# Linear attention on one core: loads of K and V in pairs of groups, and stores that wait for a load directly

## The chip, the cores and the metric

The kernel runs on one core of a Trainium2 chip. The core has five engines with instruction streams of their own: PE (matrix multiply, with its weight loads shown as PEld), DVE (vector), ACT (scalar), POOL (GpSimd) and SP (sync, which only issues transfers here). Sixteen DMA engines move data between HBM and the on-chip memory SBUF. POOL, SP and ACT each issue transfers; POOL's go to the queue q0, SP's to q1 and ACT's to q10. The metric is the device time of one execution in microseconds (us); less is better. MB below are 1,048,576 bytes where a tile is meant.

## The reference

```python
Q_feat = np.maximum(0, Q)
K_feat = np.maximum(0, K)
KV = np.einsum('bhkd,bhkv->bhdv', K_feat, V)
K_sum = np.sum(K_feat, axis=2)
numerator = np.einsum('bhqd,bhdv->bhqv', Q_feat, KV)
denominator = np.einsum('bhqd,bhd->bhq', Q_feat, K_sum)
return (numerator / (denominator[:, :, :, None] + 1e-10)).astype(np.float32)
```

Q, K, V and the result are fp32 of shape 8 x 12 x 512 x 64: 96 heads, each 512 rows of 64 numbers, 12.58 million bytes per tensor.

## The kernel before

**Tiling.** The 96 heads are cut into 12 octets of 8 heads (`NO = 12`); each octet has two groups of 4 heads. For a group, K is a tile of 128 partitions with 16 rows of 64 numbers each, so 4 KB of fp32 in one piece per partition and 512 KB in all; V likewise. For an octet, Q is a tile with 8 KB per partition, 1 MB in all, and so is the output. An octet therefore reads 3 MB by five loads (K, V, K, V, Q) and writes 1 MB by one store.

**Loads.** All loads except those of the first octet's K and V are issued by POOL (lines 92 to 100, loop at 110) and change fp32 to bf16 on the way, so they write half the bytes they read. The order on POOL is Q of octet 0, then for each octet K and V of group one, K and V of group two, and Q. The four K and V tiles of the first octet are loaded as fp32 by SP (K) and ACT (V), lines 103 to 107; they lie in two buffers of the output pool. The pools `kin` and `vin` have 12 buffers each (one group per buffer, six octets), `qin` has 7 (one octet each), and `outp` has `DELAY + 2` = 7. In the compiled program a POOL load also waits for the landing of the load eight before it, so at most eight POOL loads are under way.

**Compute.** `prep` and `prep_v` (lines 133 to 146) make masked copies of K (with relu) and V of one group on DVE and ACT; `mm_kv` (148) multiplies them on PE; `evac_kv` (156) copies the products to SBUF on ACT. `qt` (181) transposes Q on PE and applies relu on ACT. `denom` (207) and `out_t` (193) form the denominators and the numerators, `backs` (272) transposes the numerators back on PE, divides them on DVE into an output tile `o_sb` (`norm`, line 234) and calls `store`. The work is issued in the order written (`manual_schedule`), in a loop over octets (lines 286 to 301) that prepares octet o+1 while it finishes octet o and, up to octet 8, octet o-1. From `o >= SAME = 8` the order differs: octet o is finished in the same round.

**Stores.** `store(o)` (line 240) is issued by SP. It first issues a copy of one row of 64 numbers from the K tile of octet o + `DELAY` into `scratch`. That copy can't leave until this K tile has landed, and as SP issues in order, the store behind it can't either. So stores of early octets are held back until the load stream is five octets further on. The last five octets' stores have no such copy. The last octet's store is cut into two halves (line 245).

Of the kernel before, what the change touches and what calls it, by code (L numbers as in the profile page):

```python
# [10 lines left out]
def kernel(  # L11
# [7 lines left out]
    nc = tc.nc  # L19
    B, H, S, D = Q.shape  # L20
    assert D == 64
    P = 128
# [4 lines left out]
    R = S * 4 // P  # L27
# [3 lines left out]
    NG = NH // NHG  # L31
    NO = NG // 2
    assert NO * 8 == NH and R == 16 and RQ == 32
    DELAY = 5
    F32 = 2

    fp32 = mybir.dt.float32
    bf16 = mybir.dt.bfloat16
# [3 lines left out]
    def pool(name, bufs, **kw):  # L42
        return ctx.enter_context(tc.tile_pool(name=name, bufs=bufs, **kw))

    consts = pool("consts", 1)
    qin = pool("qin", 7)
    kin = pool("kin", 12)
    vin = pool("vin", 12)
    kfp = pool("kfp", 4)
    rcp = pool("rcp", 2)  # L50
    outp = pool("outp", DELAY + 2)
    otp = pool("otp", 2)
# [5 lines left out]
    def view(X, f):  # L58
        return X.rearrange("b h s d -> (b h s d)").rearrange("(n p f) -> n p f", p=P, f=f)

    Qr, Kr, Vr, Or = view(Q, RQ * D), view(K, R * D), view(V, R * D), view(out, RQ * D)
# [14 lines left out]
    kvf = [consts.tile([P, 8 * 2 * D1], bf16, name=f"kvd{i}") for i in range(NK)]  # L76
    kvd = [x.rearrange("p (h d) -> p h d", h=8) for x in kvf]
    mask = consts.tile([P, 2, 2], fp32, name="mask")
    scratch = consts.tile([1, D], bf16, name="scratch")

    mask_h = consts.tile([P, 8, 2], fp32, name="mask_h")

# [5 lines left out]
    ctx.enter_context(tc.manual_schedule())  # L88

    q_sb, k_sb, v_sb = {}, {}, {}  # L90

    def load_kv(g):
        k_sb[g] = kin.tile([P, R, D], bf16, name="k_sb")
        nc.gpsimd.dma_start(out=k_sb[g].rearrange("p r d -> p (r d)"), in_=Kr[g])  # L94
        v_sb[g] = vin.tile([P, R, D], bf16, name="v_sb")
        nc.gpsimd.dma_start(out=v_sb[g].rearrange("p r d -> p (r d)"), in_=Vr[g])  # L96

    def load_q(o):
        q_sb[o] = qin.tile([P, U, 2 * D], bf16, name="q_sb")
        nc.gpsimd.dma_start(out=q_sb[o].rearrange("p u f -> p (u f)"), in_=Qr[o])  # L100


    for g in range(F32):
        kv = outp.tile([P, 2, R, D], fp32, name="kv_first", tag="o_sb")
        k_sb[g], v_sb[g] = kv[:, 0], kv[:, 1]
        nc.sync.dma_start(out=k_sb[g].rearrange("p r d -> p (r d)"), in_=Kr[g])
        nc.scalar.dma_start(out=v_sb[g].rearrange("p r d -> p (r d)"), in_=Vr[g])
    load_q(0)
    make_identity(nc, ident)
    for o in range(1, NO):  # L110
        load_kv(2 * o)
        load_kv(2 * o + 1)
        load_q(o)

    def zero(i):
# [122 lines left out]


    def store(o, o_sb):  # L240
        if o + DELAY < NO:
            nc.sync.dma_start(out=scratch, in_=k_sb[2 * (o + DELAY)][0:1, 0, :])
        Ov = Or[o].rearrange("p (r d) -> p r d", d=D)
        if o == NO - 1:
            for j in range(2):
                rs = slice(RQ // 2 * j, RQ // 2 * (j + 1))
                nc.sync.dma_start(out=Ov[:, rs], in_=o_sb[:, rs])
            return
        nc.sync.dma_start(out=Ov, in_=o_sb)

    def out_tile():
        return outp.tile([P, RQ, D], fp32, name="o_sb", tag="o_sb")
# [19 lines left out]
    def backs(o):  # L272
        o_sb = out_tile()
        for j in range(2):
            norm(o, j, back(o, j), o_sb)
        store(o, o_sb)
# [26 lines left out]
    o = NO - 2  # L303
    g = 2 * NO - 2
# [9 lines left out]
    o_sb = out_tile()  # L314
# [4 lines left out]
    for i in range(2):  # L319
        relu_q(o + 1, i, transp(o + 1, i), nc.vector if i == 1 else None)  # L320
    norm(o, 1, ps, o_sb)
    store(o, o_sb)
    idle(5, o + 1)
    out_t(o + 1, (0,))
# [32 lines left out]
```

## Time and profile before

Three runs took 126.52, 126.65 and 126.98 us; the median is 126.65. The profiled execution has a span of 124.8 us from its first to its last instruction; the runs' times include what lies around the span.

| what | value |
|---|---|
| median of three runs | 126.65 us |
| span of the profiled execution | 124.8 us |
| read from HBM, written to HBM | 37.75 MB, 12.58 MB |
| loads of Q, K, V by POOL (q0) | 12 + 22 + 22 |
| transfers on SP: first K, small copies, stores | 2 + 7 + 13 |
| transfers on ACT: first V | 2 |
| POOL busy | 31.2 us |
| issue to landing, median: K, V, Q loads | 14.1, 13.2, 14.8 us |
| issue to landing, median: whole stores | 9.0 us |

In the profile's slices each digit is a fortieth of the span; in the windows the last three columns are the clock granted to PE, the share of the 16 DMA engines' time that had packets in it (it can exceed 1, as packets overlap), and GB/s on the side written. In a timeline the first column is the start, the second the duration, and the bracket says how long the engine stood idle before and what ended that.

### The profile page before, as it was taken

To read this page: it belongs to the slowest core of one execution; us is meant where nothing else is said; L and a number is where in the kernel's file an instruction comes from. 1 tells how busy PE (TensorE), PEld (TensorE's weight loads), DVE (VectorE), ACT (ScalarE), POOL (GpSimd) and SP (SyncE) were. 2 spreads that over 40 slices of the span, in tenths; PEclk is the share of its full clock that TensorE was granted. 3 is DMA by queue.
4 is the path that set the end of the run, shared out by engine and by line. 5 is a ranking of instruction groups with operands and counts; after the bars stand their busy time and mean duration, and the time that the engine had idled before them with its cause. 6 is when DMAs were issued, how large, how long until landed. Compare 5 with 4: busy or idle time off the path is not lost.

```text
span 124.8 us, 2656 instructions
## 1 busy us (share of the span) xinstructions
PE 86.6 (69%) x1067; PEld 78.5 (63%) x1067; DVE 81.1 (65%) x176; ACT 79.4 (64%) x114; POOL 31.2 (25%) x62
## 2 busy tenths in 40 slices
PE   0032287998889899893598599399777577797600
PEld 0031285997878787792597499299576476695500
DVE  2257644759797997989147845934928918979430
ACT  0163369989898999988149558665939737737100
POOL 6902434314243331142133115034122000000000
PEclk9999999999999999999779859959999999999995
DMA  3999999999999999999999999999999999999993
GB/s 112 377 306 215 215 205 210 217 205 218 203 215 211 206 223 324 253 216 300 281 215 280 304 213 249 331 215 230 334 234 218 323 257 215 312 421 420 428 416 143
DMA packets 10748, 32.68 MB, mean 262 GB/s; under 512 B 1392, under 2 KB 1392, under 8 KB 9328
## 3 DMA queue, kind: packets, MB, share of 16 engines
q0 software_dynamic: 8064, 17.83, 74.7%
q1 hardware_dynamic: 2384, 13.63, 27.1%
q10 hardware_dynamic: 288, 1.05, 2.2%
q8 instruction: 8, 0.13, 0.4%
q14 instruction: 4, 0.03, 0.1%
HBM read 37.75 MB, written 12.58 MB: 403 GB/s over the span
## 4 chain that ended last, share of the span: by engine, by line
DMA 34%; DVE 30%; PE 23%; ACT 5%; issue 2%; DVEq 1%; SPq 0%; POOLq 0%; ACTq 0%
DMA v_sb<-in_V_dram 14%; DVE o_sb L234 13%; DMA q_sb<-in_Q_dram 13%; PE ps_kv L150 11%; DMA kv_first<-in_K_dram 7%; PE ps_bk L228 7%; DVE kf L136 5%; PE ps_qt L171 4%; DVE vo L138 3%; ACT kvd L160 2%; DVE vo L145 2%; PE ps_ot L201 2%; DVE den L218 2%; ACT qt L179 2%; DVE rec L222 1%
## 5 line engine op out<-in xcount | busy, mean ns | idle before, releaser
L150 PE MATMUL ps_kv<-vo,kf 128*128 128x132 bf16 x384 | 30.8, 244 | 17.7 <-ACT vo L143 8.2
L150 PEld LDWEIGHTS <-kf 128*128 128x128 bf16 x384 | 28.4, 110 | 19.0 <-DVE vo L138 10.9
L234 DVE TENSOR_TENSOR o_sb<-ps_bk,rec 128x1024 f32<-128x1024 f32 x24 | 28.3, 1219 | 17.1 <-PE ps_bk L228 17.1
L160 ACT CAST kvd<-ps_kv 64x260 bf16<-64x260 f32 (+1 forms) x54 | 18.7, 346 | 19.5 <-PE ps_kv L150 16.6
L203 ACT COPY ot_sb<-ps_ot 128x1024 f32<-128x1024 f32 x24 | 24.0, 1014 | 3.0 <-PE ps_ot L201 2.0
L179 ACT ACTIVATE qt<-ps_qt 128x1024 bf16<-128x1024 bf16 x23 | 22.4, 1026 | 5.6 <-PE ps_qt L171 5.5
L228 PE MATMUL ps_bk<-ident,ot_sb 128*128 128x128 f32 x192 | 23.0, 273 | 0.4 <-ACT ot_sb L203 0.4
L136 DVE TENSOR_SCALAR kf<-k_sb,mask 128x1024 bf16<-128x1024 bf16 x44 | 18.4, 460 | 6.4 <-DMA k_sb<-in_K_dram 6.3
L94 POOL DMA_DIRECT2D k_sb<-in_K_dram x22 | 11.9, 542 | 37.7 <-DMA q_sb<-in_Q_dram 24.1
L228 PEld LDWEIGHTS ps_bk<-ident,ot_sb 128*128 128x128 f32 x192 | 20.8, 141 | 0.7 <-ACT ot_sb L203 0.7
L171 PE MATMUL ps_qt<-ident,q_sb 128*128 128x128 bf16 x192 | 16.0, 250 | 6.0 <-DMA q_sb<-in_Q_dram 5.9
L171 PEld LDWEIGHTS <-q_sb 128*128 128x128 bf16 x192 | 14.3, 114 | 7.3 <-DMA q_sb<-in_Q_dram 7.1
L201 PE MATMUL ps_ot<-qt,kvd 128*128 128x256 bf16 x96 | 14.7, 283 | 5.0 <-DVE o_sb L234 4.3
L96 POOL DMA_DIRECT2D v_sb<-in_V_dram x22 | 12.3, 558 | 17.4 <-DMA k_sb<-in_K_dram 11.1
L201 PEld LDWEIGHTS <-kvd 128*128 128x128 bf16 x96 | 9.2, 101 | 7.8 <-issue 5.7
L138 DVE TENSOR_SCALAR vo<-v_sb,mask 128x1024 bf16<-128x1024 bf16 x22 | 10.6, 482 | 1.8 <-DMA v_sb<-in_V_dram 1.8
L143 ACT ACTIVATE vo<-v_sb,mask 128x1024 bf16<-128x1024 bf16 x10 | 11.5, 1152 | 0.2
L210 PEld LDWEIGHTS <-qt 128*128 128x128 bf16 x192 | 6.8, 97 | 4.4 <-ACT qt L179 3.4
L210 PE MATMUL ps_den<-kvd,qt 128*128 128x16 bf16 x192 | 7.5, 180 | 2.4 <-ACT qt L179 2.1
L100 POOL DMA_DIRECT2D q_sb<-in_Q_dram x12 | 6.6, 546 | 8.5 <-DMA v_sb<-in_V_dram 6.2
L213 DVE SCALAR_TENSOR_TENSOR own<-ps_den,mask_h 128x256 f32<-128x256 f32 x12 | 5.0, 417 | 3.3 <-PE ps_den L210 3.3
L136 DVE TENSOR_SCALAR kf<-kv_first,mask 128x1024 bf16<-128x1024 f32 x4 | 2.8, 749 | 5.1 <-DMA kv_first<-in_K_dram 5.1
(24 smaller groups left out, 28.3 us busy)
## 6 DMA issues: line engine op xcount, KB each, us to landing
out_dram<-o_sb SPq DMA_DIRECT2D x11, 1024.0 KB, 9.0
q_sb<-in_Q_dram POOLq DMA_DIRECT2D x12, 512.0 KB, 14.8
k_sb<-in_K_dram POOLq DMA_DIRECT2D x22, 256.0 KB, 14.1
v_sb<-in_V_dram POOLq DMA_DIRECT2D x22, 256.0 KB, 13.2
kv_first<-in_V_dram ACTq DMA_DIRECT2D x2, 512.0 KB, 7.2
kv_first<-in_K_dram SPq DMA_DIRECT2D x2, 512.0 KB, 6.9
out_dram<-o_sb SPq DMA_DIRECT2D x2, 512.0 KB, 4.3
scratch<-k_sb SPq DMA_DIRECT2D x7, 0.1 KB, 5.0
```

What stands on the lines that cost most here:

```text
L96: nc.gpsimd.dma_start(out=v_sb[g].rearrange("p r d -> p (r d)"), in_=Vr[g])
L136: nc.vector.tensor_scalar(kf[g][:, :, s, :], k_sb[g], scalar1=0.0, scalar2=mask[:, 0, s:s + 1], op0=Alu.max, op1=Alu.mult)
L138: nc.vector.tensor_scalar(vo[g % NB][:, :, 0, 2:D + 2], v_sb[g], scalar1=mask[:, 1, 0:1], scalar2=None, op0=Alu.mult)
L150: nc.tensor.matmul(ps_kv[:, g % 2, 0:2 * (D + 2)].rearrange("p (t d) -> p t d", t=2), kf[g][:, r, :, :].rearrange("p s d -> p (s d)"), vo[ ...
L160: copy(kvd[o % NK][64 * c:64 * c + 64, 4 * gs.start + s:4 * gs.stop:2, c * D1:c * D1 + D1].rearrange("p (g t) d -> p g t d", t=2), ps_kv[6 ...
L171: nc.tensor.transpose(ps[:, u, :], q_sb[o][:, i * (U // 2) + u, :], ident)
L179: nc.scalar.activation(to, ps, Act.Relu)
L201: nc.tensor.matmul(ps[:, i], kvd[o % NK][:, h, 1:2 * D + 1], q[:, :, h, :], start=True, stop=True, skip_group_check=True)
L203: nc.scalar.copy(ot[o][:, :, 4 * j:4 * j + 4], ps.rearrange("p h u c -> p u h c"))
L210: nc.tensor.matmul(ps[:, u], qt_sb[o % NZ][:, u, :], kvd[o % NK][:, :, 0:2 * D1:2 * D1 - 1], start=True, stop=True, skip_group_check=True)
L228: nc.tensor.transpose(ps[:, 2 * v:2 * v + 2].rearrange("p c d -> p (c d)"), ot[o][:, 8 * j + v].rearrange("p h c -> p (h c)"), ident32)
L234: nc.vector.tensor_tensor(o_sb[:, rs], ps, rec[o][:, rs].unsqueeze(2).to_broadcast([P, 16, D]), op=Alu.mult)
```

## The change

K of the two groups of an octet is loaded by one transfer into one tile of 128 partitions by two groups, V likewise; for the first octet too, where SP issues one transfer for K and ACT one for V. The pools `kin` and `vin` have 6 buffers of twice the size. The small copy and its tile `scratch` are gone; instead `store(o)` carries a dependency on the load of K of octet o + `DELAY`. `DELAY` goes from 5 to 6, and with it `outp` from 7 buffers to 8. POOL has 34 loads instead of 56, SP 14 transfers instead of 22, ACT one instead of two.

```diff
-    DELAY = 5
-    F32 = 2
+    DELAY = 6
...
-    kin = pool("kin", 12)
-    vin = pool("vin", 12)
+    kin = pool("kin", 6)
+    vin = pool("vin", 6)
...
-    scratch = consts.tile([1, D], bf16, name="scratch")
...
-    def load_kv(g):
-        k_sb[g] = kin.tile([P, R, D], bf16, name="k_sb")
-        nc.gpsimd.dma_start(out=k_sb[g].rearrange("p r d -> p (r d)"), in_=Kr[g])
-        v_sb[g] = vin.tile([P, R, D], bf16, name="v_sb")
-        nc.gpsimd.dma_start(out=v_sb[g].rearrange("p r d -> p (r d)"), in_=Vr[g])
+    k_load = {}
+    after_load = mybir.DependencyInfo(mybir.DependencyClass.Sync, mybir.DependencyReason.DATA)
+
+    def load_pair(o, eng, tiles, X, pool, dt, name, tag=None):
+        t = pool.tile([P, 2, R, D], dt, name=name, tag=tag or name)
+        ld = eng.dma_start(out=t.rearrange("p g r d -> p g (r d)"),
+                           in_=X[2 * o:2 * o + 2].rearrange("g p f -> p g f"))
+        for i in range(2):
+            tiles[2 * o + i] = t[:, i]
+        return ld
+
+    def load_kv(o):
+        k_load[o] = load_pair(o, nc.gpsimd, k_sb, Kr, kin, bf16, "k_sb")
+        load_pair(o, nc.gpsimd, v_sb, Vr, vin, bf16, "v_sb")
...
-    for g in range(F32):
-        kv = outp.tile([P, 2, R, D], fp32, name="kv_first", tag="o_sb")
-        k_sb[g], v_sb[g] = kv[:, 0], kv[:, 1]
-        nc.sync.dma_start(out=k_sb[g].rearrange("p r d -> p (r d)"), in_=Kr[g])
-        nc.scalar.dma_start(out=v_sb[g].rearrange("p r d -> p (r d)"), in_=Vr[g])
+    load_pair(0, nc.sync, k_sb, Kr, outp, fp32, "k_first", "o_sb")
+    load_pair(0, nc.scalar, v_sb, Vr, outp, fp32, "v_first", "o_sb")
     load_q(0)
     make_identity(nc, ident)
     for o in range(1, NO):
-        load_kv(2 * o)
-        load_kv(2 * o + 1)
+        load_kv(o)
         load_q(o)
...
     def store(o, o_sb):
-        if o + DELAY < NO:
-            nc.sync.dma_start(out=scratch, in_=k_sb[2 * (o + DELAY)][0:1, 0, :])
...
-        nc.sync.dma_start(out=Ov, in_=o_sb)
+        st = nc.sync.dma_start(out=Ov, in_=o_sb)
+        if o + DELAY < NO:
+            tc.add_manual_dep(st.ins, k_load[o + DELAY].ins.name, after_load, reason="store after load")
```

## The prediction

> **What bounds the kernel now.** I read the page's 40 slices first, then the windows, then the DMA issues of POOL and SP in order of time, then the chain of waits.
>
> ```profile
> span 124.8 us, 2656 instructions
> PE 86.6 (69%) x1067; PEld 78.5 (63%) x1067; DVE 81.1 (65%) x176; ACT 79.4 (64%) x114; POOL 31.2 (25%) x62
> DMA  3999999999999999999999999999999999999993
> HBM read 37.75 MB, written 12.58 MB: 403 GB/s over the span
> ```
>
> No engine is busy for more than 69% of the span, but the DMA row is full from the second slice to the last but one. The windows (columns: us, busy time of PE, PEld, DVE, ACT, POOL, then granted clock, DMA share, GB/s) say the same by stage:
>
> ```profile
> 3.00:6.00 3.00, 0.00 (x0) 0.00 (x0) 0.50 (x1) 0.27 (x1) 3.00 (x6) 1.00 1.03 384
> 12.00:42.00 30.00, 24.54 (x313) 22.62 (x314) 21.42 (x51) 23.97 (x38) 10.50 (x20) 1.00 1.10 211
> 52.89:102.85 49.96, 38.10 (x461) 34.91 (x461) 31.44 (x60) 32.72 (x47) 11.66 (x22) 0.90 1.09 263
> 114.00:118.00 4.00, 3.45 (x37) 2.79 (x33) 2.29 (x5) 1.97 (x2) 0.00 (x0) 1.00 1.01 426
> ```
>
> The GB/s count bytes on the side written. The loads turn fp32 into bf16, so 211 in the load-only stretch is 422 read from HBM; the store-only stretch writes 426. All stretches run at the same HBM rate, so the time is a sum of bytes over that rate, plus the start and the end. POOL's timeline prices one load, because the issue of a load waits for the landing of the load eight before it on that queue:
>
> ```profile
> 34.48 0.53 POOL L94 DMA_DIRECT2D k_sb<-in_K_dram  x1 [1.68 <-DMA q_sb<-in_Q_dram]
> 35.70 0.53 POOL L96 DMA_DIRECT2D v_sb<-in_V_dram  x1 [0.69 <-DMA k_sb<-in_K_dram]
> 36.95 0.56 POOL L100 DMA_DIRECT2D q_sb<-in_Q_dram  x1 [0.72 <-DMA v_sb<-in_V_dram]
> 38.25 0.53 POOL L94 DMA_DIRECT2D k_sb<-in_K_dram  x1 [0.74 <-DMA k_sb<-in_K_dram]
> 39.48 0.53 POOL L96 DMA_DIRECT2D v_sb<-in_V_dram  x1 [0.70 <-DMA v_sb<-in_V_dram]
> 41.91 0.53 POOL L94 DMA_DIRECT2D k_sb<-in_K_dram  x1 [1.90 <-DMA q_sb<-in_Q_dram]
> ```
>
> From 34.48 to 39.48 four K and V loads of 512 KB land: 1.25 us each. The next step, 2.43 us, is one Q of 1 MB. So an octet's loads take 7.43 us, and two half-size loads cost 2 x 1.25 - 2.43 = 0.07 us more than one of the same bytes. SP's timeline gives the octet with a store in it:
>
> ```profile
> 52.89 0.51 SPq L242 DMA_DIRECT2D scratch<-k_sb  x1
> 62.89 0.50 SPq L242 DMA_DIRECT2D scratch<-k_sb  x1
> 102.85 0.50 SPq L242 DMA_DIRECT2D scratch<-k_sb  x1
> 118.47 1.46 SPq L247 DMA_DIRECT2D out_dram<-o_sb  x2
> ```
>
> Each small copy leaves when its K lands: (102.85 - 52.89) / 5 = 9.99 us an octet. A store alone is 1.0486 MB / 426 GB/s = 2.46 us. 9.99 - 7.43 - 2.46 leaves 0.10 us an octet for the small copy and for mixing reads with writes. The chain of waits, last:
>
> ```profile
> 47.20 16.97 DMA v_sb<-in_V_dram
> 64.70 16.02 DMA q_sb<-in_Q_dram
> 80.77 1.42 PE ps_qt L171 x16
> 118.44 1.13 DVEq L352
> ```
>
> Compute waits for loads up to 80.72, runs 37.7 us without a load wait, and the last store's halves are issued at 118.47 and 119.60. By the completion events they land up to 123.91, and the packet records show about 16 packets in flight up to 122.0: no gap before the last store, though little to spare.
>
> **The change part by part.** The span of this execution is 124.8 and the runs' median 126.65, so 1.85 us lie around the span; I take those as they are and subtract from 126.65.
>
> *Fewer load transfers.* K and V of octets 1 to 11 go from 44 transfers to 22 with the same bytes, in the same rows of 4 KB read and 2 KB written, so the packets of data stay and 22 completions go. One completion packet on this queue takes 0.021 us (mean of the 896 four-byte packet records), and it is on each engine's path since the queue is never empty: 22 x 0.021 = 0.46 us as the lower end. The upper end gives the whole 0.07 to the transfer: 1.54 us. Part of the 0.07 may belong to 2 KB packets, which stay. The nearest row of one transfer against two is the last store: its halves land 1.255 us apart (mean over engines) where whole stores land 2.46 apart, so splitting cost 2 x 1.255 - 2.46 = 0.05, packets included. I take the middle of 0.021 and 0.05, 0.035: 22 x 0.035 = 0.77 us.
>
> By the Trainium skill (DMA: Bandwidth & Descriptors, "Anatomy of one DMA") a POOL-issued transfer has a fixed cost of about 2.0 us; taken serially, 22 fewer would save 44 us. The 1.25 us between landings here is less than that alone, so with eight in flight the fixed part is hidden, and the sum goes by the rows.
>
> *First octet.* Two transfers on SP and two on ACT become one and one: 2 x 0.02 = 0.04 us (0 to 0.14). Prep of group 0 now waits for both groups. It began at 5.50 and the second group's at 10.25, with about 2.8 us of VectorE work between. If the pair lands as late as the second group did, compute starts its steady run 2.8 us later; if at 7.3, nothing is late. What is late next is prep of octets 1 to 5, at 7.2 us an octet in the chain against 7.43 of loads and later 9.99; the load waits between 47 and 81 us (PE's weight loads 7.1 us on Q, VectorE 4.6 us on K) take it up. So 0. Uncovered it costs up to 2.8 us at the end.
>
> *The small copy.* Seven go. Each put one 8-byte packet (0.036 us mean) and a completion (0.023) on each engine: 7 x 0.059 = 0.41 us. Bounds: 0 if they fit between other packets, and 7 x 0.10 = 0.70, the whole remainder of a mixed octet.
>
> *Waits and order.* A store now waits itself for the K pair of the octet six later. Behind it on SP stand only later stores; for them wait only the o_sb buffers. With eight, two of them lent to the first octet, norm of octet 8 needs store 0. Store 0 will leave when the K pair of octet 6 lands: 52.89 less one store (2.56) plus half a pair (1.25), about 51.5, and lands by 57 (5 us beside loads). Norm of octet 8 ran at 94.2: over 35 us of cover. All loads from octet 6 on come about 2.5 us earlier, as one store more stays for the end: order, no bytes. One store fewer is mixed with loads: 0.04 us at most, taken. At the end compute moves with Q of octet 8 (80.72 to about 77.6), so the last store is issued near 116.5, ahead of the backlog; each later stall in compute has some 3 us of cover.
>
> *POOL.* Its loads keep their order; 22 issues of about 0.55 us go, and a pair writes twice the packets (0.53 to 1.1 us each by one or two of today's issues). It is 25% busy and eight transfers, now 8 MB, are queued ahead: 0. Buffers: K of octet 7 needs prep of octet 1 (near 24 us, or 27) and would be issued near 36.
>
> *Reading the pair.* Each engine now steps between two regions 512 KB apart, which no row of before does. Bounds: the mixed octets step between read and write streams and lose at most 0.10 of 9.99, 1%; the stretch 3 to 6 us, with K and V of the first octet read from two queues, ran at 406 GB/s on the HBM side by the packet records against 422, 3.8% less, a start-up stretch. Over 44 x 1.25 = 55 us that is 0.55 to 2.1 us lost; nothing is the other end, since Q's longer rows and the K rows differ by only 0.07 a megabyte. I take nothing, as the packets and their sizes stay.
>
> The same page ("Latency and other measured facts") speaks against this: copies whose rows lie 512 KiB apart ran at 207 GB/s per direction instead of 214. Applied to the 55 us that is an estimated loss of 1.8 us, and the sum would turn into a loss of about 0.6. No run shows it yet, and here only pairs of rows lie so far apart.
>
> Sum: 0.77 + 0.04 + 0.41 + 0.04 = 1.26 us; 126.65 - 1.26 = 125.4. Own range: 126.65 - 0.46 = 126.2 down to 126.65 - (1.54 + 0.14 + 0.70 + 0.04) = 124.2.
>
> **The rivals.** A measurement of this kernel tells about 0.5% (0.63 us) from no change, so the line is at 126.0.
>
> *Hidden anyway.* Completions and copies overlap the data: the packet records sum to 1.10 times the DMA time in the load stretch, so records overlap. Then 0.1 to 0.6 us is gained, about 126.3. Against: the 0.10 and 0.07 us are differences of landings, not of records.
>
> *Paired reads run slower* (ends slower). Price 2.1 us less 1.26: 127.5. It decides from 1.26 / 55 = 2.3% on. For: the 3.8% above. Against: that stretch starts up.
>
> *The late start reaches the end* (slower too). If the 2.8 us is not taken up, the last half store is issued at 122.4; its first packet came 1.0 us after issue, its data need 1.25 and the landing some 0.7, so it lands near 125.4 instead of 123.91: 128.1. It decides once the last issue is later than about 119.7. Against: the load waits before 81 us.
>
> That the wait does not do its work is excluded: in the compiled program each of the first six stores waits on a load's completion.
>
> **How the numbers follow.** Forecast, below 126.0: 0.60. Hidden, 126.0 to 127.2: 0.22. Slower reads 0.12, late start 0.06. So faster 0.60, same 0.22, slower 0.18. The time is the forecast's, 125.4. The range goes from 124.2 to 127.2, which takes in the hidden case and leaves most of the two slow ones out; the forecast's own is 124.2 to 126.0.
>
> **What would show it.** Right: K and V pairs land 2.43 to 2.46 us apart where two halves took 2.50; stores leave just under 9.95 us apart, the first near 51; the DMA row stays full; the last store is issued two or three us before it can move. Wrong: pairs 2.55 or more apart (slower reads), or a digit under 9 in the last slices and a last issue after 119.7 (late start).

## The result

The changed kernel takes 127.09 us (median of 7 runs, 126.89 to 127.19) against 126.67 (7 runs, 126.52 to 126.98): a ratio of 1.003, 95% interval 1.0018 to 1.0041. It is slower by 0.4 us, with an interval that leaves out 1, and by less than the half per cent that was named as the limit; 125.4 was forecast. The profiled execution took 127.0 us and has a span of 125.2.

The page of the changed kernel, for comparison with the four lines shown of before:

```profile
span 125.2 us, 2614 instructions
...
PE 85.0 (68%) x1067; PEld 76.9 (61%) x1067; DVE 81.0 (65%) x176; ACT 79.0 (63%) x114; POOL 23.7 (19%) x40
...
DMA  3999999999999999999999999999999999999991
...
HBM read 37.75 MB, written 12.58 MB: 402 GB/s over the span
```

The bytes are the same, and the DMA row is as full up to the last slice. Its windows, of the start first and then the three stretches of before (columns as there):

```profile
0.00:3.00 3.00, 0.00 (x0) 0.00 (x0) 0.77 (x15) 0.00 (x0) 1.89 (x8) 1.00 0.37 81
3.00:6.00 3.00, 0.00 (x0) 0.00 (x0) 0.00 (x0) 0.00 (x0) 3.00 (x6) 1.00 1.02 363
...
12.00:42.00 30.00, 23.65 (x307) 22.04 (x308) 22.49 (x56) 25.31 (x39) 7.57 (x12) 1.00 1.10 212
52.89:102.85 49.96, 39.44 (x480) 35.52 (x478) 32.30 (x63) 35.21 (x52) 6.12 (x10) 0.90 1.08 263
114.00:118.00 4.00, 3.27 (x28) 2.62 (x26) 2.29 (x5) 1.73 (x2) 0.00 (x0) 1.00 1.02 428
```

```profile
0.00:3.00 3.00, 0.00 (x0) 0.00 (x0) 0.76 (x15) 0.00 (x0) 1.89 (x9) 1.00 0.33 100
```

The second fence is the kernel before. From 12 us on the rates are those of before within 0.5%; the first 3 us move 81 instead of 100 GB/s, and 3 to 6 us 363 instead of 384. POOL's timeline prices the new loads as it did the old ones, each issue leaving when the load eight before has landed:

```profile
16.38 0.70 POOL L94 DMA_DIRECT2D k_sb<-in_K_dram  x1 [1.90 <-DMA v_sb<-in_V_dram]
18.81 0.71 POOL L94 DMA_DIRECT2D v_sb<-in_V_dram  x1 [1.73 <-DMA q_sb<-in_Q_dram]
21.28 0.56 POOL L106 DMA_DIRECT2D q_sb<-in_Q_dram  x1 [1.76 <-DMA k_sb<-in_K_dram]
23.83 0.76 POOL L94 DMA_DIRECT2D k_sb<-in_K_dram  x1 [1.99 <-DMA v_sb<-in_V_dram]
26.27 0.71 POOL L94 DMA_DIRECT2D v_sb<-in_V_dram  x1 [1.67 <-DMA q_sb<-in_Q_dram]
```

The steps to 18.81 and to 26.27 are a Q: 2.43 and 2.44 us, as before. The steps to 21.28 and 23.83 are a pair of K and one of V: 2.47 and 2.55. Two half loads took 2.50, so a pair gains next to nothing. By the landings themselves (completion events, mean over engines, loads that land from 12.5 to 47 us) a pair takes 2.50 us and two half loads took 2.52.

Where did the 0.4 us go? I took two things from each profiled execution: the last landing of a transfer (completion events), and the bytes moved on the HBM side by 12 and by 115 us (packet records).

| | before | after |
|---|---|---|
| MB moved by 12 us | 3.935 | 3.821 |
| MB moved from 12 to 115 us | 43.00 | 43.21 |
| last store lands, mean over engines | 123.22 | 123.03 |
| last store lands, slowest engine | 123.91 | 123.89 |
| from there to the end of the span | 0.91 | 1.32 |

At 0.42 MB/us the start loses 0.27 us and the stream gains 0.50. The mean landing gains about the difference, 0.19; the slowest engine, which ends the program, gains 0.02, and why it gains no more is open. The whole loss lies behind the last landing, in the closing instructions; what lies around the span is 1.8 us in both kernels. This is the view of POOL's instructions on the line of the launch from 124.3 us on (duration min/median/max in ns, then first and last start); before, then after:

```profile
L352 POOLq DRAIN  x2: 45/74/102, 124.2 to 124.6; - x2
L352 POOLq EVENT_SEMAPHORE  x2: 17/17/17, 124.6 to 124.7; - x2
```

```profile
L354 POOLq DRAIN  x2: 45/69/93, 124.3 to 124.6; - x2
L354 POOLq EVENT_SEMAPHORE  x2: 17/17/17, 125.0 to 125.1; - x2
```

The last drain starts at 124.6 in both. Before, the next instruction follows at once; after, it starts 0.4 us later, and all engines wait for it.

### The profile page after: what moved, and what is told of

Its sections match the earlier page's. It is cut to its first block, busy times and chain, and to the rows that moved or that the text cites. A ratio compares the mean times of both kernels' runs of the same rounds, so it can differ in the third digit from the quotient of the medians.

```text
span 125.2 us, 2614 instructions
## 1 busy us (share of the span) xinstructions
PE 85.0 (68%) x1067; PEld 76.9 (61%) x1067; DVE 81.0 (65%) x176; ACT 79.0 (63%) x114; POOL 23.7 (19%) x40
## 4 chain that ended last, share of the span: by engine, by line
DVE 37%; DMA 28%; PE 19%; ACT 7%; issue 3%; DVEq 1%; ACTq 0%
DMA v_sb<-in_V_dram 20%; DVE o_sb L236 15%; PE ps_kv L152 10%; DMA k_first<-in_K_dram 7%; DVE kf L138 7%; PE ps_bk L230 7%; DVE vo L140 4%; ACT kvd L162 3%; DVE vo L147 3%; DVE den L220 2%; PE ps_qt L173 2%; DVE rec L224 2%; DVE own L215 2%; ACT qt L181 2%; ACT vo L145 1%
## 5 line engine op out<-in xcount | busy, mean ns | idle before, releaser
L152 PE MATMUL ps_kv<-vo,kf 128*128 128x132 bf16 x384 | 30.2, 240 | 19.9 <-ACT vo L145 13.8
L152 PEld LDWEIGHTS <-kf 128*128 128x128 bf16 x384 | 27.4, 107 | 21.6 <-DVE vo L140 12.9
L173 PE MATMUL ps_qt<-ident,q_sb 128*128 128x128 bf16 x192 | 14.7, 237 | 0.7 <-DMA q_sb<-in_Q_dram 0.7
L173 PEld LDWEIGHTS <-q_sb 128*128 128x128 bf16 x192 | 13.3, 108 | 1.4 <-DMA q_sb<-in_Q_dram 1.3
L94 POOL DMA_DIRECT2D v_sb<-in_V_dram x11 | 8.2, 750 | 22.2 <-DMA q_sb<-in_Q_dram 9.4
L106 POOL DMA_DIRECT2D q_sb<-in_Q_dram x12 | 7.1, 588 | 20.9 <-DMA k_sb<-in_K_dram 15.3
L94 POOL DMA_DIRECT2D k_sb<-in_K_dram x11 | 7.9, 717 | 15.4 <-DMA v_sb<-in_V_dram 9.8
L138 DVE TENSOR_SCALAR kf<-k_first,mask 128x1024 bf16<-128x1024 f32 x4 | 2.8, 750 | 7.7 <-DMA k_first<-in_K_dram 7.7
```

The lines of the kernel that those rows point to most:

```text
L94: ld = eng.dma_start(out=t.rearrange("p g r d -> p g (r d)"), in_=X[2 * o:2 * o + 2].rearrange("g p f -> p g f"))
L138: nc.vector.tensor_scalar(kf[g][:, :, s, :], k_sb[g], scalar1=0.0, scalar2=mask[:, 0, s:s + 1], op0=Alu.max, op1=Alu.mult)
L152: nc.tensor.matmul(ps_kv[:, g % 2, 0:2 * (D + 2)].rearrange("p (t d) -> p t d", t=2), kf[g][:, r, :, :].rearrange("p s d -> p (s d)"), vo[ ...
L173: nc.tensor.transpose(ps[:, u, :], q_sb[o][:, i * (U // 2) + u, :], ident)
```

## The experiments

All times are medians. Each ratio, with its 95% interval, is to runs of the old kernel beside them on the same chip, whose medians lay between 126.67 and 126.83; so times of different rows are best compared by their ratios. "End" is the time from the last landing to the end of the span.

| run | what | us | ratio | interval | last norm ends | last landing | end |
|---|---|---|---|---|---|---|---|
| before | | 126.67 | | | 119.57 | 123.91 | 0.91 |
| after | | 127.09 | 1.0030 | 1.0018 to 1.0041 | 119.34 | 123.89 | 1.32 |
| e1_pad | after, 40 memsets on POOL | 126.61 | 0.9992 | 0.9983 to 1.0001 | 118.32 | 123.79 | 0.97 |
| e2_first | after, first octet in four loads | 127.21 | 1.0035 | 1.0023 to 1.0047 | 119.16 | 123.74 | 1.70 |
| e3_dep | before, dependency for the copy | 127.62 | 1.0097 | 1.0060 to 1.0133 | 120.61 | 124.37 | 1.33 |
| e4_pair | before, pairs alone | 127.19 | 1.0057 | 1.0030 to 1.0083 | 120.52 | 124.27 | 1.28 |
| e5_delay6 | before, DELAY 6 alone | 126.66 | 0.9995 | 0.9986 to 1.0005 | 116.47 | 123.90 | 0.96 |
| e6_qpiece | after, Q in 4 KB pieces | 127.46 | one run | | 118.71 | 124.17 | 1.48 |
| e8_behind | e3 with copies behind stores | 127.05 | 1.0050 | 1.0021 to 1.0080 | 121.50 | 125.25 | 0.90 |
| e9_lane | before, one copy more | 127.45 | 1.0053 | 1.0038 to 1.0069 | 120.61 | 124.33 | 1.33 |
| e10_best | e1 with first K in two loads | 126.25 | 0.9963 | 0.9949 to 0.9978 | 118.33 | 123.89 | 0.92 |
| e11_pad8 | e10 with 8 memsets | 126.28 | 0.9949 | 0.9929 to 0.9969 | 117.66 | 123.77 | 0.92 |
| e12_whole | e1, four first loads, last store whole | 126.40 | 0.9962 | 0.9945 to 0.9979 | 118.17 | 123.57 | 0.91 |
| e13_delay5 | e12 with DELAY 5 | 128.24 | 1.0111 | 1.0091 to 1.0131 | 121.08 | 125.87 | 0.91 |

The last three columns are of one profiled execution each, which can lie away from the median of its kernel (e10's took 126.58, e8's 127.94).

### The end of POOL's stream

```diff
         load_q(o)
+    pad = consts.tile([P, 1], fp32, name="pad")
+    for i in range(40):
+        nc.gpsimd.memset(pad, 0.0)
```

> The changed kernel with 40 memsets of one number per partition on POOL behind its last load (near 83 us, nothing waits for them). Theory: the changed kernel's transfers end where the old one's did (123.9 us), and its extra 0.4 us lies behind the last landing, in POOL's last instructions, because POOL's instruction stream became some 32 instructions shorter and now meets a stop at its very end; then the padding moves the stop away, the time from the last landing to the end falls from 1.3 to 0.9 us, and the median from 127.09 to about 126.7. Rival: the 0.4 us come from the pair transfers or from the order of the stores, whatever POOL's length; then the end stays 1.3 us long and the median 127.1.

126.61, close to the theory's 126.7: 0.48 us less for 40 memsets that nothing needs, and an end of 0.97 us. The same view of this kernel:

```profile
L357 POOLq EVENT_SEMAPHORE  x2: 17/17/17, 124.6 to 124.7; - x2
L357 POOLq DRAIN  x1: 45/45/45, 124.5 to 124.5; - x1
```

The drain starts at 124.5 and the next instruction at 124.6 again. With 8 memsets instead of 40 (the base is e10):

> The fastest version so far (K of the first octet in two loads, memsets behind POOL's loads) with 8 memsets instead of 40. Theory: the 0.4 us stop sits at a fixed place of POOL's instruction stream, and its last handful of instructions lie on it by chance; then 8 instructions move it too, the end after the last landing is 0.9 us and the median 126.25. Rival: it takes some 32 instructions, as many as the old kernel had more; then the end is 1.3 us and the median 126.65.

126.28 with an end of 0.92 us: 8 are enough, if e10 without memsets has the stop, which was not run (e2, which differs from it in the first load of V alone, has it). So the stop depends on where POOL's closing instructions come to lie, not on pairs or on the stores. The traces place it: in all four kernels with the stop (after, e2, e4, e6) it lies between the 68th and the 69th instruction that the profile records on POOL. The first three have 70 there, e6 has 71, and so in e6 the stop comes one closing instruction earlier, ahead of the last drain:

```profile
L356 POOLq EVENT_SEMAPHORE_RANGE_CLEAR  x1: 140/140/140, 124.7 to 124.7; - x1
L356 POOLq DRAIN  x2: 102/142/182, 124.6 to 125.2; - x2
```

The clear ends at 124.84 and the drain starts at 125.24. The ten kernels without the stop have 78 to 110 instructions there, so their 69th runs long before the end. What happens at this place is only hinted at. The instruction queue q14 fetches 8 KB at 70.7 us in the old kernel, at 86.1 with 40 memsets and at 85.9 with 8, and in every kernel without the stop between 68 and 89 us; in the four with the stop that fetch comes at 125.7 to 126.0, behind the stop. That a stop goes with the crossing of a block of instructions fits this; it was not tried by itself.

### The completion counters that SP waits for

```diff
-    load_pair(0, nc.sync, k_sb, Kr, outp, fp32, "k_first", "o_sb")
-    load_pair(0, nc.scalar, v_sb, Vr, outp, fp32, "v_first", "o_sb")
+    for g in range(2):
+        kv = outp.tile([P, 2, R, D], fp32, name="kv_first", tag="o_sb")
+        k_sb[g], v_sb[g] = kv[:, 0], kv[:, 1]
+        nc.sync.dma_start(out=k_sb[g].rearrange("p r d -> p (r d)"), in_=Kr[g])
+        nc.scalar.dma_start(out=v_sb[g].rearrange("p r d -> p (r d)"), in_=Vr[g])
```

> The changed kernel with the first octet's K and V in four loads as before. Theory: a pair takes twice as long to be set up, so V's first packet starts at 3.07 us instead of 2.16 and the DMA engines lose about 0.27 us at the start, which nothing gives back; then V's first packet is back near 2.2 us, and the median falls by 0.2 to 0.3 us, to about 126.85. Rival: the start is regained later, as other queues fill the gap; then the median stays at 127.1 (and the late prep of group 0 has no price either).

127.21, where the theory had 126.85 and the rival 127.1. The start came back (V's first packet at 2.18, 3.96 MB by 12 us), and the last landing is 0.15 us earlier than in the changed kernel; but the end grew to 1.70 us. Transfers of SP and ACT take eight completion counters in turn, and at the end SP waits for them in a fixed order, 0.06 us a wait. With two transfers more the last store is on the first of the eight, so seven waits that could have been done earlier follow the last landing, six more than in the changed kernel, and the stop is there as well. The next run tests that on the old kernel, by one small copy more:

```diff
+        if o + DELAY == NO:
+            nc.sync.dma_start(out=scratch, in_=k_sb[2 * NO - 2][0:1, 0, :])
         if o + DELAY < NO:
```

> The old kernel with one small copy more, ahead of the store of octet 7 (which no load holds back any more), so that the last store moves from the last of the eight completion counters to the first. Theory: SP's waits behind the last landing grow from 0.06 to about 0.5 us, and the median from 126.67 to 127.1. Rival: one more copy and its counter change nothing: 126.7.

127.45: more than the theory's 127.1, but the end is 1.33 us as it says. SP's instructions on the launch line from 123.5 us on, before and then with the copy:

```profile
L352 SPq EVENT_SEMAPHORE  x3: 17/17/28, 123.9 to 124.8; - x3
```

```profile
L354 SPq EVENT_SEMAPHORE  x10: 17/28/28, 124.3 to 125.6; - x10
```

Seven waits more stand behind the last landing (123.91 and 124.33). They make 0.42 of the 0.70 us that the median lies above that of the old kernel's runs beside it. In the profiled execution the last norm is 1.0 us later as well, and the clock granted to PE was halved between 100.3 and 103.8 us; what makes the other 0.28 us of the median was not separated.

### The dependency and the small copy

```diff
-        if o + DELAY < NO:
-            nc.sync.dma_start(out=scratch, in_=k_sb[2 * (o + DELAY)][0:1, 0, :])
...
+        st = nc.sync.dma_start(out=Ov, in_=o_sb)
+        if o + DELAY < NO:
+            tc.add_manual_dep(st.ins, k_load[2 * (o + DELAY)].ins.name, after_load, reason="store after load")
```

> The old kernel with the dependency instead of the small copy, DELAY 5, 7 buffers, single loads. The prediction's term: 7 x 0.059 = 0.41 us less, 126.26. Theory after the result: the spacing of stores fell only from 9.99 to 9.94 us, so 7 x 0.02 to 0.05, 126.35 to 126.55. Rival: nothing, as the copy's packets fit between others: 126.67.

127.62 (127.47 to 128.89): a loss of 0.92 us against the old kernel's runs beside it, which none of the three expectations had. Of it 0.42 are the counters (the last store is on the first again: the end is 1.33). The stream moved 43.02 MB from 12 to 115 us against 43.00, so the copies themselves cost 0.05 us, not 0.41. The rest goes with late compute. Q of octet 8 lands at 81.91 instead of 80.72, and the last norm ends at 120.61 instead of 119.57. The stores leave some 0.25 us earlier, as no copy stands in front of them (53.20 instead of 53.45 for the second), so they probably come ahead of more of the next Q's packets; that was not tested by itself, but e8 below, whose stores leave as early, has this Q as late (81.81), and e9, whose copies lead, has not (80.44). These are SP's last issues in this kernel, and the DMA's windows at its end:

```profile
103.18 12.54 SPq L248 DMA_DIRECT2D out_dram<-o_sb  x5
119.51 1.46 SPq L246 DMA_DIRECT2D out_dram<-o_sb  x2
```

```profile
118.00:120.00 2.00, 1.09 (x10) 0.85 (x8) 1.75 (x2) 0.00 (x0) 0.00 (x0) 1.00 0.94 397
120.00:122.00 2.00, 0.00 (x0) 0.00 (x0) 0.61 (x1) 0.00 (x0) 0.00 (x0) 1.00 0.92 377
```

Before, the first half left at 118.47; here at 119.51, and the DMA share drops under 1 ahead of it. So the old kernel stood at the edge: 1 us later in compute, and the engines are no longer full before the last store. To part the two losses, the copies were put back behind their stores, which gives the last store the last counter:

```diff
             tc.add_manual_dep(st.ins, k_load[2 * (o + DELAY)].ins.name, after_load, reason="store after load")
+            nc.sync.dma_start(out=scratch, in_=k_sb[2 * (o + DELAY)][0:1, 0, :])
```

> The dependency alone as in the run before, but with the seven small copies kept, now behind their stores, so the stores leave as early as in that run and the last store has the last of the eight completion counters again. Theory: of the 0.9 us that the dependency alone lost, 0.43 are SP's waits at the end (seven waits of 0.06 us after the last landing, as the last store had the first counter) and 0.46 the late Q loads and last norm (120.6 against 119.6), so the waits fall away and the rest stays: 127.2, last norm near 120.6. Rival: the waits cost nothing, as the barrier hides them: 127.6. If the copies cost the prediction's 0.059 us each, 0.41 comes on top.

127.05, with an end of 0.90: the counters' part is gone. The runs spread from 126.69 to 128.54, and the profiled one, with a last norm at 121.50, is among the slower, so the part of compute is not the fixed 0.46 us of the theory. The stream (43.01 MB) shows no price of the copies.

### Pairs alone, DELAY alone, and both

> The old kernel with K and V of octets 1 to 11 in pairs, all else as before (small copies, DELAY 5, first octet in four loads). The prediction's term: 22 x 0.035 = 0.77 us less, 125.9. Theory after the result: pairs land 2.49 us apart where two halves took 2.50, so 0.0 to 0.3 us are gained, and POOL's shorter stream puts its stop of 0.4 us at the end: 126.8 to 127.1, with 1.3 us from the last landing to the end. Rival: the pairs gain nothing and the end stays 0.9 us: 126.67.

The edit is the pair loads of the change for octets 1 to 11, and nothing else. 127.19, a little above the 126.8 to 127.1 of the theory, with the stop at the end (1.28 us) as expected. The stream gains 0.33 us (43.14 MB), which is 0.015 a pair. But the last norm ends at 120.52 and the runs spread from 126.96 to 128.51: V of an octet's first group now lands with the second's, and the last wait in the chain is for a V (it ends at 86.36).

> The old kernel with DELAY 6 and 8 buffers alone (small copies and single loads stay). Theory: in the old kernel the last store is issued just when the DMA engines run dry (last norm ends 119.57), and with one store more held back the loads come 2.5 us earlier and the last norm ends near 117; the transfers were not waiting for it, so their end moves by at most 0.3 us, and the last store, now on the completion counter that SP waits for last but one, costs 0.06 us: 126.4 to 126.7. Rival: the end of compute sets the end, and the time falls by 1 us or more: under 125.7.

126.66: the last norm ends 3.1 us earlier, and the time is the same. Transfers, not compute, set the old kernel's end, if only just.

> The run before with DELAY 5 and 7 buffers. Theory: V of an octet's first group now lands with its pair, some 2.5 us later within the octet's loads, and without the store held back once more the last norm ends near 120.5, after the engines run dry: 0.3 to 1.5 us more than with DELAY 6, and scatter, as in the run with pairs alone. Rival: DELAY 6 is not needed: the same time.

The base is e12, below; its only edit is DELAY 5, and with it 7 output buffers instead of 8. 128.24 instead of 126.40, more than the 0.3 to 1.5 us expected: with pairs, holding back the sixth store is what keeps compute off the path. The windows of this kernel's end show the transfers running out before the last store:

```profile
118.00:120.00 2.00, 1.56 (x15) 1.32 (x13) 1.28 (x2) 0.00 (x0) 0.00 (x0) 1.00 0.88 373
120.00:122.00 2.00, 0.00 (x0) 0.00 (x0) 1.08 (x1) 0.00 (x0) 0.00 (x0) 1.00 0.22 90
122.00:124.00 2.00, 0.00 (x0) 0.00 (x0) 0.00 (x0) 0.00 (x0) 0.00 (x0) 1.00 1.02 414
```

From 120 to 122 us the engines are 22% busy while DVE finishes the last norm.

### What a shorter piece costs

```diff
-        q_sb[o] = qin.tile([P, U, 2 * D], bf16, name="q_sb")
-        nc.gpsimd.dma_start(out=q_sb[o].rearrange("p u f -> p (u f)"), in_=Qr[o])
+        t = qin.tile([P, 2, U + 2, D], bf16, name="q_sb")
+        t = t.rearrange("p h u d -> p h (u d)")
+        nc.gpsimd.dma_start(out=t[:, :, 0:U * D], in_=Qr[o].rearrange("p (h f) -> p h f", h=2))
...
```

The instructions that read Q follow its new shape, and `qin` has 6 buffers instead of 7.

> The changed kernel with each Q still loaded by one transfer of 1 MB, but in two pieces of 4 KB per partition instead of one of 8 KB (a gap in the tile keeps them apart; qin has 6 buffers). Theory: what two half loads cost more than one Q, 0.07 us, belongs to the shorter pieces and not to the completions, so Q now takes as long as a pair, 2.49 us instead of 2.45, and the twelve Qs cost up to 0.5 us. Rival (the prediction's): it belongs to the completions; then Q stays at 2.44 to 2.45 us.

POOL's timeline of this kernel:

```profile
16.27 0.71 POOL L94 DMA_DIRECT2D k_sb<-in_K_dram  x1 [1.75 <-DMA v_sb<-in_V_dram]
18.73 0.72 POOL L94 DMA_DIRECT2D v_sb<-in_V_dram  x1 [1.75 <-DMA q_sb<-in_Q_dram]
...
23.74 0.72 POOL L94 DMA_DIRECT2D k_sb<-in_K_dram  x1 [1.81 <-DMA v_sb<-in_V_dram]
26.21 0.71 POOL L94 DMA_DIRECT2D v_sb<-in_V_dram  x1 [1.75 <-DMA q_sb<-in_Q_dram]
```

A Q now takes 2.46 and 2.47 us where it took 2.43 and 2.44, with the same bytes and one completion: 0.03 us for shorter pieces. Twelve of them are 0.36 us, and from 12 to 115 us this kernel moved 43.08 MB against 43.21, a loss of 0.31 us. The one time taken, 127.46, is 0.37 over the changed kernel, but 0.2 when each is taken beside its own old kernel, and the end is 0.16 longer, so the time adds nothing. So about half of the 0.07 us that two half loads cost more than one Q seems to belong to their 4 KB pieces, which a pair keeps; it rests on one profile, and a price of the missing buffer was not parted from it.

### A version that beats both

```diff
-    load_pair(0, nc.sync, k_sb, Kr, outp, fp32, "k_first", "o_sb")
+    k_first = outp.tile([P, 2, R, D], fp32, name="k_first", tag="o_sb")
+    for g in range(2):
+        k_sb[g] = k_first[:, g]
+        nc.sync.dma_start(out=k_sb[g].rearrange("p r d -> p (r d)"), in_=Kr[g])
```

> The changed kernel with the 40 memsets behind POOL's loads and with K of the first octet in two loads (V stays a pair), which puts the last store on the last completion counter. Theory: 126.61 less 0.06 (counter) less 0.1 to 0.25 (V's first packet near 2.2 us instead of 3.07): 126.3 to 126.45, which beats both kernels. Rival: the start is not worth anything: 126.55.

V stays a pair. With the memsets of e1 this gives 126.25, 0.9963 of the old kernel (0.9949 to 0.9978) and 0.84 us less than the changed one. The number is just under the theory's 126.3 to 126.45, but its reason is not shown: V's first packet came at 2.82 (in e11, with the same first loads, at 2.51) instead of 3.04, and 3.83 MB were moved by 12 us, hardly more than in the changed kernel. Beyond the counter's 0.06 us, the cause of its 0.36 us over e1 stays open.

> The changed kernel with 40 memsets behind POOL's loads, the first octet in four loads as before, and the last octet's store whole, which keeps the last store on the last completion counter. Theory: the start is 0.2 to 0.3 us better than with pairs, and the last store, issued 1.1 us later than its first half was, still finds transfers ahead of it (last norm near 118.3, engines dry near 121): 125.9 to 126.25. Rival: the whole store starts too late and the engines stand idle before it: 126.6 or more.

The edit is the four first loads of e2 with the memsets, and the branch that halves the last store taken out. 126.40 (126.08 to 126.84), above the theory's 126.25 and under the rival's 126.6, and not told apart from e10 and e11. The last store, issued at 118.19, still found transfers ahead of it.

## Why the prediction was wrong

Two steps failed. The one that turned the sign is the term *POOL*, "0", with the sum's silence on the stretch from the last landing to the end of the span. (The 1.85 us around the span, which were taken as they are, did stay: 1.8.) The change took 22 issues off POOL and so put POOL's closing instructions where a stop of 0.4 us lies; e1 and e11 end without it, with memsets. It also gave the last store another counter, 0.06 us. Together that stretch grew from 0.91 to 1.32 us. Without both the changed kernel would stand near 126.55 (an estimate: e1's 126.61 less 0.06), 0.1 us under the old one.

The other step makes the larger part of the 1.7 us between 125.4 and 127.09: of the 1.26 us that the sum takes off, the stream and the start together gave 0.23, and the last landing 0.02. Three terms were mis-sized, as told below; the two largest priced completions and copies as time on each engine's path (completions "since the queue is never empty"), and measured 0.33 of 0.77 and 0.05 of 0.41. That 127.09 still lies under the 127.2 of the range is luck: the range reaches there for a case that gains.

*Fewer load transfers, 0.77 us.* Mis-sized: the stream gained 0.33 with pairs alone, 0.015 a pair. That is less than even the lower end, 0.46, from the completion packets. The half stores that moved me up carry shorter pieces too, and e6 points to 0.03 us a megabyte for these, on loads.

*The small copy, 0.41 us.* Mis-sized: 0.05 in e3, and nothing in e8. Under pairs, leaving it out is worth up to the 0.17 us between e4 and the changed kernel. The 0.10 us left over in a mixed octet was therefore mostly something else: mixing, or the error of the three prices it was left over from; which was not shown.

*First octet, a gain of 0.04 us.* It was a loss. The late prep was taken up as said, but the transfers also start late: V's first packet came at 3.04 us instead of 2.16. By 12 us the three kernels with both first loads as pairs (after, e1, e6) had moved 3.77 to 3.82 MB, the nine with four first loads 3.85 to 3.97: about 0.1 MB, some 0.25 us.

*Order and cover.* Store 0 left at 51.74, where 51.5 was worked out, and octets follow at 9.94 us, just under 9.95. Q of octet 8 landed at 77.76, where 77.6 was worked out. But the last norm did not move three us ahead with it. With singles it does (e5, 116.47); with pairs it waits for V of the pair, which is late in its octet. The chain of waits of the changed kernel shows it:

```profile
58.43 25.54 DMA v_sb<-in_V_dram
...
84.40 2.35 DVE o_sb L236 x2
...
98.65 1.55 PE ps_kv L152 x16
100.20 1.71 PE ps_qt L173 x16
101.90 1.26 PE ps_bk L230 x8
...
118.20 1.13 DVEq L354
```

The wait ends with V of octet 9 at 84.0, where before it ended with Q of octet 8 at 80.7. So pairs spend most of the time that DELAY 6 gains; e13 shows what pairs cost without it, 1.8 us. About 1 us more goes with the clock in this execution: that granted to PE was halved from 99.1 to 102.5 us, and the three PE steps above took 4.52 us, where in e1, with the same transfers and a full clock there, they took 2.89, and the last norm ended 1.0 us earlier, at 118.32.

*Reading the pair: nothing taken.* Right: pairs land 2.50 us apart by the mean over engines, no slower than two halves (2.52). That lies between the two signs that were named, 2.43 to 2.46 for right and 2.55 for slower reads. The estimate of 1.8 us from the Trainium skill (DMA: Bandwidth & Descriptors, "Latency and other measured facts"), whose row is of copies between HBM tensors, did not come about here. Beside the sum, such a loss would have left 0.54 us, not 0.6.

*Hidden anyway* was the rival nearest to what the stream did: it gained 0.5 us. Had I taken that and left the end alone, 126.3 would have been forecast, and the sign would still have been wrong.

## What to carry to other kernels

In this kernel, whose transfers are busy from first to last, removing a transfer without removing bytes was worth one or two hundredths of a microsecond; look at once at what else the removed instructions were holding in place. Tenths lay behind the last landing: count the waits that follow the last transfer's counter, and look there for a gap on any engine whose instruction count changed. A loss of a few tenths after an edit is no verdict on the edit until that part of the span has been compared.

## What the runs showed of the hardware

Forty memsets of one number per partition, done 35 us before the end, made the changed kernel faster by 0.48 us (e1, 126.61 against 127.09), and with eight the end is as short (e11, 0.92 us). The stop that they move away lies between the 68th and the 69th recorded instruction of POOL in all four kernels that have it.

SP's closing waits take 0.06 us each, and the number of its and ACT's transfers modulo eight decided how many of them stood behind the last landing. Without the stop, the end is 0.90 to 0.92 us with 24 or 16 transfers (before, e8, e10 to e13), 0.96 or 0.97 with 23 or 15 (e5, e1) and 1.33 with 25 or 17 (e9, e3).

With the first K and V in one transfer of 1 MB each, all issued at 0.74 us, V's first packet on ACT's queue came at 3.04 to 3.07 us (after, e1, e6), against 2.14 to 2.50 in the nine kernels with four transfers of 512 KB; with K alone in two it came at 2.51 and 2.82 (e11, e10). Whether K's transfer or V's own length holds it back was not separated.
